# Keeping the four matmuls of a modulation product together in TensorE's order

## The chip, the core and the metric

The kernel runs on one core of a Trainium2 chip. The metric is the device time of one execution in microseconds. Three runs of the kernel before took 3296.96, 3298.60 and 3299.93 us, a median of 3298.6 us. A further execution was taken with the hardware profiler; all rows below are of that one.

## What is computed

The reference runs two blocks of two layers each on 256 latent and 256 context tokens of width 2048: sliding-window attention and latent attention (MLA) in the first block, a mixer of pooling and an RWKV recurrence and then full attention in the second. Each of the four layers is modulated by a condition vector. For the latent tokens it is `c`, for the context tokens `c_ctx`:

```python
shift, scale, gate = jnp.split(cond @ ada_w[i] + ada_b[i], 3, axis=-1)      # cond = silu(c), width 2048
h = rmsnorm(x, norm_g[i]) * (1.0 + scale) + shift
x = x + gate * o                                                            # o: the layer's mixer
```

(In the second block the weights are `mod_w`, and the norm stands elsewhere.) The change concerns only the product `cond @ ada_w[i]`: two condition vectors of 2048 by a 2048 x 6144 matrix, four times, in fp32.

## The kernel before, in words

**The modulation.** The 6144 columns of a layer are cut into 12 groups of 512, and the 2048 rows into four parts `q` of 512 rows. One part of one group is a tile `mraw` of 128 partitions x 4 x 512 numbers (1 MB), so there are 4 x 12 x 4 = 192 tiles, loaded by 192 DMAs on SP's queue (L240) into three buffers. For each tile TensorE does four matmuls (L260), one for each `j` in 0 to 3. Their stationary operand `cs` has just 32 columns, of which two hold the two conditions, and each writes its own band of 32 partitions of one PSUM bank `mv`; `tile_position=(0, 32 * j)` gives each its own quarter of the columns of TensorE's array. I call the four matmuls of one tile a quad. The trace shows two records for each fp32 matmul: 768 matmuls, 1536 records, eight for a quad. After the last quad of a batch ScalarE copies the bank (`ev`, L267), four small matmuls (L273) sum the bands and turn them, and VectorE adds the bias (`mod`, L279).

**When it runs.** `mod_steps` is a generator; each `next` does one quad. `fill`, called after every weight tile of the big products, takes as many steps as a rate (`PACE`) says, and `need` takes the missing ones before a layer uses its modulation. So quads are strewn over the program, between the matmuls of the layers.

**The big products.** `mm3` multiplies in three parts (L352, L353, L354) of 128 x 512, with weights that ScalarE and VectorE split into a rounded part `whi` (L323) and a rest `wlo` (L324). Their raw tiles are loaded on SP's queue too (L338), in the order of that queue. A recurrence in the RWKV mixer (`chain`, L1418 to L1444) alternates between TensorE and ScalarE or VectorE: each step of it needs what they made of the step before.

**What sets the order.** The program is written once in Python, and a scheduler then orders the instructions of each engine by a simulated run: of those that it holds ready, the one that was written earliest goes first. Engines work through their order strictly, and waits are semaphores. So the four matmuls of a quad stand together in TensorE's order only where nothing that was written earlier became ready, in the simulated run, while they were being placed. In the order before, 151 of the 192 quads stand together and 41 are broken: 40 into two pieces (mostly the first matmul alone and then the three others), one into three. So TensorE comes back for the rest of a quad 42 times.

Of the kernel before, what the change touches and what calls it, by code (L numbers as in the profile page):

```python
# [116 lines left out]
class Net:  # L117
# [125 lines left out]
    def mod_steps(self):  # L243
        nc = self.nc
        for i in range(4):
            if i % 2 == 0:
                self.conditions(i // 2)
            mod, cs = self.mod[i], self.cs
            for gs in MOD_BATCHES[min(i, 1)]:
                pb = self.bank("mv")  # L250
                for n, g in enumerate(gs):
                    for q in range(4):
                        while len(self.mod_ahead) < (self.mod_pool[1] - 1 if self.mod_pool and self.mod_loads else 0):
                            self.mod_load()
                        if not self.mod_ahead:
                            self.mod_load()
                        raw = self.mod_ahead.pop(0)
                        for j in range(4):
                            k = 4 * q + j
                            nc.tensor.matmul(  # L260
                                pb[32 * j : 32 * j + 32, :], cs[:, 32 * k + 30 - 2 * n : 32 * k + 62 - 2 * n], raw[:, j, :],
                                start=(n == 0 and q == 0), stop=(n == len(gs) - 1 and q == 3), tile_position=(0, 32 * j),
                            )
                        self.mod_wait = MOD_LAG
                        yield
                ev = self.t512("ev")
                nc.scalar.copy(ev, pb)  # L267
                for _ in range(MV_LAG):
                    yield
                p2 = self.bank("mv2")  # L270
                c = 2 * len(gs)
                for j in range(4):
                    nc.tensor.matmul(  # L273
                        p2[:, c * j : c * j + c], ev[:, j * P : (j + 1) * P], self.sel[:, :c], start=True, stop=True
                    )
                for n, g in enumerate(gs):
                    bias = self.v("mod_b", i * 48 + g * 4, 4).unsqueeze(2).broadcast_to([P, 4, 2])
                    pv = p2[:, : 4 * c].rearrange("p (j n c) -> p j n c", j=4, c=2)[:, :, n, :]
                    nc.vector.tensor_tensor(mod[:, g * 4 : (g + 1) * 4, :], pv, bias, op=ALU.add)  # L279
                    self.mod_done.add((i, g))  # L280
                yield
# [1759 lines left out]
```

## Time and profile before

| | |
|---|---|
| median of three runs | 3298.6 us |
| profiled execution | 3288.34 us, its span 3286.3 us |
| TensorE matmul busy | 3117.3 us, 95% of the span |
| VectorE, ScalarE, GpSimd busy | 2101.0, 1481.1, 351.2 us |
| L260 matmul records | 1536 |
| TensorE's granted clock, mean | 0.983 of full |

"Busy" is the time in which at least one instruction of the engine is at work. Matmuls are pipelined, so a record's own duration is longer than the time after which the next one starts; where a cost is wanted, the start of one row is to be compared with the start of the next. "PEld" is the loading of the stationary operand, "SPq" is SP's queue of DMAs, "idle before" is time in which an engine waited, and behind the arrow stands what ended it.

### The profile page before, as it was taken

To read this page: it belongs to the slowest core of one execution; us is meant where nothing else is said; L and a number is where in the kernel's file an instruction comes from. 1 tells how busy PE (TensorE), PEld (TensorE's weight loads), DVE (VectorE), ACT (ScalarE), POOL (GpSimd) and SP (SyncE) were. 2 spreads that over 40 slices of the span, in tenths; PEclk is the share of its full clock that TensorE was granted. 3 is DMA by queue.
4 is the path that set the end of the run, shared out by engine and by line. 5 is a ranking of instruction groups with operands and counts; after the bars stand their busy time and mean duration, and the time that the engine had idled before them with its cause. 6 is when DMAs were issued, how large, how long until landed. Compare 5 with 4: busy or idle time off the path is not lost. (4 is left out here: it accounts for less than half of the span.)

```text
span 3286.3 us, 53227 instructions
## 1 busy us (share of the span) xinstructions
PE 3117.3 (95%) x19762; PEld 2397.2 (73%) x19762; DVE 2101.0 (64%) x4647; ACT 1481.1 (45%) x3233; POOL 351.2 (11%) x536
## 2 busy tenths in 40 slices
PE   5999999999988999999999999999999999899997
PEld 2567777767777788897776676666677768678897
DVE  2446454553376666666777788777787546857766
ACT  2424444442276666653334334333343323646664
POOL 0000000000001111000122222221121101200000
PEclk8999999999999999999999999999999999999999
DMA  8843444348654666766434433334434474543454
GB/s 303 309 165 135 139 137 157 125 174 290 234 165 142 226 208 226 253 228 211 126 98 133 124 125 116 111 103 149 126 109 154 168 253 130 172 140 129 143 180 153
DMA packets 270771, 556.07 MB, mean 169 GB/s; under 512 B 122928, under 2 KB 150704, under 8 KB 244912
## 3 DMA queue, kind: packets, MB, share of 16 engines
q1 hardware_dynamic: 270512, 552.68, 50.8%
q8 instruction: 155, 2.54, 0.3%
q14 instruction: 104, 0.85, 0.1%
HBM read 517.46 MB, written 35.13 MB: 168 GB/s over the span
## 5 line engine op out<-in xcount | busy, mean ns | idle before, releaser
L324 DVE TENSOR_TENSOR wlo<-raw,whi 128x512 fp32r<-128x512 f32 (+2 forms) x1000 | 660.3, 668 | 572.7 <-ACT whi L323 538.3
L352 PE MATMUL a<-hhi,whi 128*128 128x512 f32 (+1 forms) x2752 | 972.8, 355 | 16.6 <-ACT whi L323 11.9
L323 ACT CAST whi<-raw 128x512 fp32r<-128x512 f32 (+2 forms) x1000 | 593.0, 599 | 815.4 <-PE a L353 470.8
L353 PE MATMUL a<-hlo,whi 128*128 128x512 f32 (+1 forms) x2752 | 947.3, 345 | 0.0
L354 PE MATMUL a<-hhi,wlo 128*128 128x512 f32 (+1 forms) x2752 | 940.0, 347 | 4.5 <-DVE wlo L324 4.3
L352 PEld LDWEIGHTS a<-hhi,whi 128*128 128x128 f32 x2752 | 525.6, 191 | 145.2 <-issue 45.0
L354 PEld LDWEIGHTS a<-hhi,wlo 128*128 128x128 f32 x2752 | 522.6, 191 | 63.5 <-DVE wlo L324 10.2
L353 PEld LDWEIGHTS a<-hlo,whi 128*128 128x128 f32 x2752 | 526.3, 191 | 46.0 <-issue 2.2
L456 POOL TENSOR_TENSOR rs<-st,mhalf 128x4 f32<-128x4 f32 (+3 forms) x109 | 145.7, 1337 | 1683.3 <-DVE st L453 1666.3
L260 PE MATMUL mv<-mraw,cs 128*32 128x512 f32 x1536 | 258.3, 629 | 16.5 <-DMA mraw<-mod_w 16.2
L352 PE MATMUL a<-whi,hhi 128*128 128x512 f32 (+1 forms) x672 | 260.6, 398 | 13.4 <-ACT sq L613 5.9
L353 PE MATMUL a<-wlo,hhi 128*128 128x512 f32 (+1 forms) x672 | 262.7, 391 | 1.4 <-DVE wlo L324 1.1
L354 PE MATMUL a<-whi,hlo 128*128 128x512 f32 (+1 forms) x672 | 258.8, 388 | 0.0
L1427 POOL TENSOR_SCALAR SD<-SV,DL 64x64 f32<-64x64 f32 x224 | 130.0, 580 | 468.7 <-DVE SV L1438 452.4
L352 PEld LDWEIGHTS a<-whi,hhi 128*128 128x128 f32 x672 | 126.1, 190 | 71.2 <-issue 18.6
L353 PEld LDWEIGHTS a<-wlo,hhi 128*128 128x128 f32 x672 | 127.9, 190 | 31.5 <-DVE wlo L324 7.3
L354 PEld LDWEIGHTS a<-whi,hlo 128*128 128x128 f32 x672 | 127.6, 190 | 25.4 <-issue 0.8
L565 ACT ACTIVATE pr<-sc,nm 128x512 f32<-128x512 f32 (+1 forms) x128 | 81.1, 633 | 90.2 <-DVE nm L562 66.7
L1430 ACT COPY SV<-chain 64x64 f32<-64x64 f32 x128 | 26.6, 208 | 184.5 <-DVE SV L1429 178.8
L556 DVE TENSOR_REDUCE mx<-sc 128x1 f32<-128x512 f32 (+1 forms) x128 | 78.9, 617 | 37.8 <-PE sc L766 15.9
L260 PEld LDWEIGHTS mv<-mraw,cs 128*32 128x32 f32 x1536 | 37.0, 110 | 87.8 <-issue 50.3
L1444 ACT COPY y<-chain 64x64 f32<-64x64 f32 x256 | 52.9, 207 | 98.2 <-PE chain L1441 87.8
(379 smaller groups left out, 4690.6 us busy)
## 6 DMA issues: line engine op xcount, KB each, us to landing
mraw<-mod_w SPq DMA_DIRECT2D x192, 1024.0 KB, 4.9
raw<-od_in SPq DMA_DIRECT2D x88, 512.0 KB, 3.6
raw<-swa_in SPq DMA_DIRECT2D x72, 512.0 KB, 3.6
raw<-ev_rkv SPq DMA_DIRECT2D x64, 384.0 KB, 3.4
raw<-ev_in SPq DMA_DIRECT2D x48, 512.0 KB, 3.9
raw<-swa_out SPq DMA_DIRECT2D x40, 512.0 KB, 5.6
raw<-ev_out SPq DMA_DIRECT2D x40, 512.0 KB, 3.6
raw<-mla_g SPq DMA_DIRECT2D x64, 256.0 KB, 3.3
```

The costliest lines, as they stand in the source:

```text
L260: nc.tensor.matmul(pb[32 * j : 32 * j + 32, :], cs[:, 32 * k + 30 - 2 * n : 32 * k + 62 - 2 * n], raw[:, j, :], start=(n == 0 and q == 0), ...
L323: nc.scalar.copy(whi, raw)
L324: nc.vector.tensor_tensor(wlo, raw, whi.bitcast(F32), op=ALU.subtract)
L352: mm(out, ah, bh, start=first, stop=False, skip_group_check=shared)
L353: mm(out, ah, bl, start=False, stop=False, skip_group_check=shared)
L354: mm(out, al, bh, start=False, stop=last, skip_group_check=shared)
L456: self.nc.gpsimd.tensor_tensor(dst, stv, mv, op=ALU.pow)
L556: nc.vector.reduce_max(mx, sc, axis=AX.X)
L565: nc.scalar.activation(pr[:, :n], sc, AF.Exp, scale=scale, bias=nm, accum_out=sm)
L1427: nc.gpsimd.tensor_scalar(SD[r_], SV[r_, hh, c, :], DL[r_, c : c + 1], None, ALU.mult)
L1430: nc.scalar.copy(SV[half[1], 1, c, :], ps[half[1], P : P + L])
L1444: nc.scalar.copy(y[r_, c, :], blk(3 * P, hh))
```

## The change

```diff
                         for j in range(4):
                             k = 4 * q + j
-                            nc.tensor.matmul(
-                                pb[32 * j : 32 * j + 32, :], cs[:, 32 * k + 30 - 2 * n : 32 * k + 62 - 2 * n], raw[:, j, :],
-                                start=(n == 0 and q == 0), stop=(n == len(gs) - 1 and q == 3), tile_position=(0, 32 * j),
-                            )
+                            with self.tc.high_priority(0 if j == 0 else None):
+                                mm = nc.tensor.matmul(
+                                    pb[32 * j : 32 * j + 32, :], cs[:, 32 * k + 30 - 2 * n : 32 * k + 62 - 2 * n], raw[:, j, :],
+                                    start=(n == 0 and q == 0), stop=(n == len(gs) - 1 and q == 3), tile_position=(0, 32 * j),
+                                )
+                                if j:
+                                    self.tc.keep_in_program_order(mm)
```

No instruction is added or taken away. `high_priority(0)` leaves the first matmul of a quad where it was; `high_priority(None)` gives the three others the priority of the program's very start, so that nothing else goes ahead of them once they may go; `keep_in_program_order` puts each behind the matmul that was written just ahead of it, an order alone, without a wait. In the order after, all 192 quads stand together. Lines below the change have numbers higher by four (L352 is L356 there), and the matmul of the modulation is L262.

The first place is on TensorE, in the first attention layer, where a quad (`mv<-mraw`) stood on both sides of a triple of a big product (`a<-whi`). Before:

```order
L354 MATMUL a_303_1677<-whi_308_1683,hlo_79 128x512
L260 MATMUL mv_161_967<-mraw_258_1549,cs_28_185 32x512
L352 MATMUL a_304_1678<-whi_308_1683,hhi_78 128x512
L353 MATMUL a_304_1678<-wlo_309_1684,hhi_78 128x512
L354 MATMUL a_304_1678<-whi_308_1683,hlo_79 128x512
L260 MATMUL mv_161_967<-mraw_258_1549,cs_28_185 32x512 x3
L352 MATMUL a_303_1677<-whi_310_1703,hhi_78 128x512
```

After:

```order
L358 MATMUL a_303_1677<-whi_308_1683,hlo_79 128x512
L262 MATMUL mv_161_967<-mraw_258_1549,cs_28_185 32x512 x4
L356 MATMUL a_304_1678<-whi_308_1683,hhi_78 128x512
L357 MATMUL a_304_1678<-wlo_309_1684,hhi_78 128x512
L358 MATMUL a_304_1678<-whi_308_1683,hlo_79 128x512
L356 MATMUL a_303_1677<-whi_310_1703,hhi_78 128x512
```

The three have moved ahead of the triple, to the first; all else stands as it did.

The second place is on TensorE in the RWKV layer, among the steps of the recurrence (`chain`). Before:

```order
L1432 MATMUL chain_5356_25845<-SV_5296_25434,BKs_5276_25358 128x128
L260 MATMUL mv_5246_25167<-mraw_5362_25881,cs_2058_9283 32x512
L1441 MATMUL chain_5356_25845<-SV_5296_25434,qb1_14957 128x128
L260 MATMUL mv_5246_25167<-mraw_5362_25881,cs_2058_9283 32x512 x3
L352 MATMUL a_5287_25391<-hhi_78,whi_5374_25972 128x512
L353 MATMUL a_5287_25391<-hlo_79,whi_5374_25972 128x512
L1418 MATMUL chain_5356_25845<-SV_5296_25434,AQ_5216_24983 128x128
```

After:

```order
L1436 MATMUL chain_5356_25845<-SV_5296_25434,BKs_5276_25358 128x128
L262 MATMUL mv_5246_25167<-mraw_5362_25881,cs_2058_9283 32x512 x4
L1445 MATMUL chain_5356_25845<-SV_5296_25434,qb1_14957 128x128
L356 MATMUL a_5287_25391<-hhi_78,whi_5374_25972 128x512
L357 MATMUL a_5287_25391<-hlo_79,whi_5374_25972 128x512
L1422 MATMUL chain_5356_25845<-SV_5296_25434,AQ_5216_24983 128x128
```

Between the chain's step L1441 and its next, L1418, there are now two matmuls instead of five.

The scheduler's simulated run comes out a little differently, and so other rows move too. The third place is on SP's queue in the RWKV layer: loads of the modulation (`mraw`) and of the layer's weights (`raw`). Before:

```order
L338 DMA raw_4008_18626<-ev_rkv 128x768
L240 DMA mraw_3994_18553<-mod_w 128x2048
L240 DMA mraw_4039_18777<-mod_w 128x2048
L1188 DMA tl_4018_18685<-lora_14738 128x512
L1188 DMA tl_4019_18686<-lora_14738 128x512
L1488 DMA oscr_80<-yo_3606_16536 128x512
L240 DMA mraw_4077_18964<-mod_w 128x2048
```

After:

```order
L240 DMA mraw_3994_18553<-mod_w 128x2048
L240 DMA mraw_4039_18777<-mod_w 128x2048
L240 DMA mraw_4077_18964<-mod_w 128x2048
L1192 DMA tl_4018_18685<-lora_14738 128x512
L1492 DMA oscr_80<-yo_3606_16536 128x512
L1192 DMA tl_4019_18686<-lora_14738 128x512
L240 DMA mraw_4119_19211<-mod_w 128x2048
L1297 DMA nscr_3999_18577<-NT_3981_18474 64x8x64
L342 DMA raw_4008_18626<-ev_rkv 128x768
```

Four loads of the modulation now stand ahead of the weights `raw_4008`; `mraw_4119` stood 21 instructions further back before. This is the largest such move on SP; over the whole program 13 of the 192 loads move by more than two places, 7 by more than five.

## Rows read from the trace of the kernel before

**Rows 1.** The core's row: span and mean granted clock

```profile
core 0: 3286.3 us, clock 0.983
```

**Rows 2.** The page: TensorE's busy time, share of the span, records

```profile
PE 3117.3 (95%) x19762; PEld 2397.2 (73%) x19762; DVE 2101.0 (64%) x4647; ACT 1481.1 (45%) x3233; POOL 351.2 (11%) x536
```

**Rows 3.** The page: the chain that ended last, shares by engine

```profile
PE 27%; DVE 5%; ACT 2%; DMA 1%; issue 1%; POOL 1%; SPq 0%; POOLq 0%; DVEq 0%; ACTq 0%
```

**Rows 4.** Two stretches: length, busy time by engine (records), clock, DMA share, GB/s

```profile
230.00:720.00 490.00, 482.36 (x2429) 357.97 (x2428) 260.49 (x652) 220.72 (x486) 17.05 (x16) 1.00 0.41 139
...
1500.00:2400.00 900.00, 869.54 (x6200) 614.62 (x6199) 697.27 (x1619) 340.86 (x860) 193.24 (x334) 0.98 0.41 125
```

**Rows 5.** Costliest groups, matmuls and weight loads: busy, mean ns | idle before, releaser

```profile
L260 PE MATMUL mv<-mraw,cs 128*32 128x512 f32 x1536 | 258.3, 629 | 16.5 <-DMA mraw<-mod_w 16.2
...
L260 PEld LDWEIGHTS mv<-mraw,cs 128*32 128x32 f32 x1536 | 37.0, 110 | 87.8 <-issue 50.3
```

**Rows 6.** Timeline, a quad that stands together: start us, own duration, records

```profile
226.99 1.06 PE L260 MATMUL mv<-mraw,cs 128*32 128x512 f32 x8
227.98 0.50 PE L352 MATMUL a<-whi,hhi 128*128 128x512 f32 x1
```

**Rows 7.** Timeline, the first broken quad, in the first attention layer

```profile
243.68 0.40 PE L354 MATMUL a<-whi,hlo 128*128 128x512 f32 x1
244.00 1.04 PE L260 MATMUL mv<-mraw,cs 128*32 128x512 f32 x2
244.98 0.50 PE L352 MATMUL a<-whi,hhi 128*128 128x512 f32 x1
245.31 0.39 PE L353 MATMUL a<-wlo,hhi 128*128 128x512 f32 x1
245.54 0.40 PE L354 MATMUL a<-whi,hlo 128*128 128x512 f32 x1
245.87 1.06 PE L260 MATMUL mv<-mraw,cs 128*32 128x512 f32 x6
246.86 0.50 PE L352 MATMUL a<-whi,hhi 128*128 128x512 f32 x1
```

**Rows 8.** Timeline, a broken quad among the steps of the recurrence

```profile
2580.23 1.04 PE L260 MATMUL mv<-mraw,cs 128*32 128x512 f32 x2
2581.21 0.49 PE L1441 MATMUL chain<-SV,qb 128*128 128x128 f32 x2
2581.63 1.06 PE L260 MATMUL mv<-mraw,cs 128*32 128x512 f32 x6
2582.61 0.50 PE L352 MATMUL a<-hhi,whi 128*128 128x512 f32 x1
2582.96 0.40 PE L353 MATMUL a<-hlo,whi 128*128 128x512 f32 x1
2583.19 0.38 PE L1418 MATMUL chain<-SV,AQ 128*128 128x128 f32 x2
2583.33 0.48 PE L354 MATMUL a<-hhi,wlo 128*128 128x512 f32 x1
```

**Rows 9.** Timeline, a broken quad while the clock was at half

```profile
2366.59 1.91 PE L260 MATMUL mv<-mraw,cs 128*32 128x512 f32 x2 [1.03 <-DMA mraw<-mod_w]
2368.43 0.79 PE L1270 MATMUL gram<-AQ,BK 64*128 64x128 f32 x2
```

**Rows 10.** Timeline, TensorE and ScalarE: a chain step and the copies of its result

```profile
1807.16 0.49 PE L1441 MATMUL chain<-SV,qb 128*128 128x128 f32 x2
...
1807.68 0.42 ACT L1444 COPY y<-chain 64x64 f32<-64x64 f32 x2 [1.67 <-PE chain L1441]
```

**Rows 11.** TensorE's waits: us in total, times, longest

```profile
PE a L352 <- ACT whi L323: 13.9, 12, 3.4
...
PE chain L1418 <- ACT y L1444: 4.2, 13, 0.6
```

**Rows 12.** Waits of SP's queue: us in total, times, longest

```profile
SPq L240 <- PE mv L260: 680.5, 163, 16.4
```

## The prediction

> **What bounds the kernel now.** I read the core's row first: one core, a span of 3286.3 us, the clock at 0.983 of full on the mean [rows 1]. The page's busy times then show TensorE at work for 3117.3 us, 95% of the span; the next, VectorE, has 64% [rows 2]. The chain that ended last agrees: of the shares that it puts to an engine, TensorE has 27 points and the next one 5 [rows 3]. A share of a whole program hides stages, so I cut it: in the first attention layer, 230 to 720 us, TensorE is busy for 482.4 of 490 us; in most of the RWKV layer, 1500 to 2400, for 869.5 of 900, with VectorE at 697.3 [rows 4]. So in the first of them nearly nothing but TensorE's own work sets the time, and in the second it does so too, but with 30.5 us of waits and with a VectorE that is not far behind. What TensorE is spared is worth its time unless it turns into a wait.
>
> **What a piece of a quad costs.** The modulation's matmuls are busy for 258.3 us; a record's mean of 629 ns times 1536 would be 966 us, so they overlap nearly four deep [rows 5]. How, the timeline shows. In a quad that stands together the eight records are done within 1.06 us, and the next matmul starts 227.98 - 226.99 = 0.99 us after the first [rows 6]. In the first broken quad the lone matmul holds TensorE for 244.98 - 244.00 = 0.98 us, and the three others for 246.86 - 245.87 = 0.99 us [rows 7]. One quarter of the array costs as much as four. Joining the two pieces saves one of them.
>
> It saves the way there and back as well. Between matmuls of the big product starts are 245.54 - 245.31 = 0.23 us apart; into the lone matmul it takes 244.00 - 243.68 = 0.32, and from the matmul behind it to the next 245.31 - 244.98 = 0.33 [rows 7]. So a visit costs 0.32 + 0.98 + 0.33 - 2 x 0.23 = 1.17 us.
>
> The page's row gives 258.3 us of busy time for these matmuls, and the rows of the timeline give the start of whatever comes next. The Trainium skill (Trainium Kernel Development and Optimization, Performance Expectations) calls matmul busy time a bad metric, because matmuls are pipelined. By busy time a visit would be worth the lone record's 1.04 us, and 42 of them 43.7 us; from start to start they are 49.1. The trace agrees with the rule here, and I use starts.
>
> Against the whole idea stands another rule. The rows show one quarter at 0.98 us and four at 0.99. The Trainium skill (TensorE: Matmul & The Clock Gate, The mechanism) says that a weight load overlaps with running matmuls only if its group of rows differs, and the four matmuls of a quad use the same rows. By that rule the loads of the three that join, six records of 110 ns [rows 5], would stand in the open, 0.66 us for each rest, and 49.1 us would shrink by 42 x 0.66 to 21.4. The trace disagrees, since 0.99 us leaves no room for them; 49.1 stays.
>
> **The sum.** No instruction comes or goes; 41 broken quads with 42 rests become 41 whole ones. The rests, counted in the order and found again in the timeline, are 11 in the first attention layer (the first of them in [rows 7]), 3 in the MLA layer, and 28 from 1526 us on, in the RWKV layer and its end.
>
> *The 14 in the first two layers.* Big matmuls stand on both sides, and waits are rare: 14 x 1.17 = 16.4 us.
>
> *The 28 in the RWKV layer.* Nineteen of the rests stand next to a step of the recurrence. There a visit costs more. In [rows 8], from the chain's L1441 to the big matmul behind the rest it takes 2582.61 - 2581.21 = 1.40 us, and from that to the next 0.35. Without the rest the first would be as from a chain step to a big matmul, 2583.33 - 2583.19 = 0.14, and the second 0.23: a saving of 1.38, less 0.01 for the larger quad ahead, 1.37 us. 19 x 1.37 = 26.0, and the nine others 9 x 1.17 = 10.5. One rest ran at half clock, behind the lone matmul of [rows 9], which took 1.84 us instead of 0.98: another 0.9. Sum 37.4 us.
>
> *What comes late next.* Of these 37.4 us a part turns into waits, since the rest was the cover for a copy. After L1441, ScalarE copies its result in two pieces that end 1807.68 + 0.42 - 1807.16 = 0.94 us after its start [rows 10], and the chain's next step L1418 needs them. In the order after, two big matmuls stand between: 0.14 + 0.23 + 0.23 = 0.60 us. So L1418 waits for 0.34 us or a little more, say 0.4, where before it seldom waited: 13 times, 4.2 us in all [rows 11]. While it waits, everything behind it on TensorE waits, since the engine goes strictly by its order. I take 0.4 for each of the 28, since the nine others stand in a layer with waits of the same kind: 11.2 us. This term is the least known. Its bounds are 0 (the scheduler has put other work into the gap) and all 37.4 (every rest was a cover for something that is due no sooner); 0.4 is what the nearest row gives.
>
> *What moves besides.* SP's queue has waited for these very matmuls for 680.5 us in 163 waits, since a load must wait for the last matmul on its buffer [rows 12]; the last one now comes sooner, so this wait shrinks. Behind it stand the weights. TensorE waits for split weights for 13.9 us in all [rows 11], so a little may be gained there; I put it at nothing, as its cover, a TensorE with other work to do, stays. The first matmul of a quad waits for the same load as before, and the three tied to it need nothing that the first did not; the ties add no wait. The other moves in the order, some hundreds of places by a few rows, I put at nothing, with either sign.
>
> Total: 16.4 + 37.4 - 11.2 = 42.6 us, so 3288.3 us of the profiled execution becomes 3245.7. The median of the runs lies 10.3 us above the profiled execution, and I carry this over: 3298.6 - 42.6 = 3256.0 us. The likeliest case has its own range of some 10 us to either side, for the size of the waits and the moved rows: 3246 to 3266.
>
> **The rivals.**
>
> *All of it is kept* (0.14). The scheduler filled each gap that it made, and nothing waits: 16.4 + 37.4 = 53.8 us, 3245 us. For it: TensorE has big matmuls in store in nearly every stretch. Against it: the second place shown of the order has nothing new between L1441 and L1418.
>
> *The RWKV layer gives nothing back* (0.16). The recurrence, not TensorE's sum of work, paces that layer, and each rest taken out becomes a wait of its size. Then only the 14 count: 3298.6 - 16.4 = 3282 us. For it: VectorE at 697 of 900 us and 30.5 us of waits [rows 4]. Against it: those waits are 3.4% of the layer; a layer paced by the recurrence would show more.
>
> *The clock* (0.03). The quads' records fill TensorE's time, and with fewer of them the gaps before chain steps widen. The clock fell to half behind a 1.03 us wait in [rows 9]; on the mean 0.983 [rows 1] is 3286.3 x 0.017 x 2 = 112 us at half, which cost 56. To eat 43 us, time at half would have to grow by three quarters: no change, 3298. Against it: a 1 us wait is not rare, and most of them left the clock alone.
>
> *The three are joined and it does not count* (0.02): the order is as wanted but the chip does not run them beside each other: 3298. The 151 quads that already stand together speak against it.
>
> *Weights held up on SP* (0.05), the slower one. Its place is the third one shown of the order: four loads of the modulation ahead of `raw_4008`, and a few like it in the same layer. If `mraw_4119` waits on its buffer, until the quad of `mraw_3994` is done, all weights behind it wait as long; the longest such wait was 16.4 us [rows 12]. TensorE then runs out of split weights. Three of these in the open cost 49.2 us: 3256.0 + 49.2 = 3305 us. It decides from the third on, since 2 x 16.4 is less than 42.6. Against it: 680.5 us of such waits stood beside just 13.9 us of TensorE's waits for weights [rows 11], so nearly none was in the open.
>
> **How the numbers follow.** The likeliest case has 0.60. Its time is the forecast: 3256 us. The range runs from 3244, just under the case where all is kept, to 3282, where the RWKV layer gives nothing; outside lie the clock, the unjoined quads and SP's queue (0.10 together) and the third of the two edge cases that overshoots (0.10). A measurement of this kernel can tell about 0.2%, 6.6 us, from no change. Faster by more: the first three cases, 0.90. Within it: 0.05, from the clock and the quads that do not overlap. Slower: 0.05, from SP's queue.
>
> **What would show it.** The modulation's matmul row must fall from 258.3 us busy by some 42 us with the same 1536 records, and the timeline must show them by eights, 0.99 us to the next start, in the RWKV layer too. In the first attention layer the work from 230 to 720 us must end some 12 us sooner, 11 x 1.17. TensorE's waits for `y` (L1444) and the other copies of the recurrence must grow, by about 11 us. I am wrong if the modulation's busy time falls and the span does not, with the waits grown by as much (the second rival), if waits for `whi` grow by tens of microseconds (SP), or if the mean clock falls to about 0.97.

## The result, and the profile after

| | before | after |
|---|---|---|
| median of the runs | 3298.2 us (4) | 3262.0 us (4) |
| lowest to highest | 3297.0 to 3299.9 | 3257.4 to 3263.0 |
| profiled execution, its span | 3288.34, 3286.3 us | 3257.43, 3255.6 us |
| records of the modulation's matmuls | 1536 | 1536 |

The kernel became 36.2 us faster, a ratio of 0.9887 [0.987, 0.9904]. Run once more at the end, beside other kernels, it took 3266.0 us against 3296.2, a ratio of 0.99 [0.9887, 0.9914]. The forecast was 3256 us, with 3244 to 3282 as its range. Gains below are worked out from the ratios, times the runs of before, and brackets hold 95% intervals.

The first lines of the page after, which answer to [rows 1 to 3], and the modulation's row, which answers to [rows 5]:

```profile
core 0: 3255.6 us, clock 0.982
...
PE 3080.4 (95%) x19762; PEld 2391.1 (73%) x19762; DVE 2102.0 (65%) x4647; ACT 1479.0 (45%) x3233; POOL 346.8 (11%) x536
...
PE 20%; DVE 3%; DMA 1%; ACT 1%; issue 1%; POOL 0%; SPq 0%; POOLq 0%; ACTq 0%; DVEq 0%
...
L262 PE MATMUL mv<-mraw,cs 128*32 128x512 f32 x1536 | 214.4, 634 | 18.9 <-DMA mraw<-mod_w 18.8
```

The reader is to see four things. The number of records is the same. The modulation's busy time fell by 258.3 - 214.4 = 43.9 us. TensorE's as a whole fell by 3117.3 - 3080.4 = 36.9. And what TensorE doesn't work, span less busy, rose from 169.0 to 175.2 us. The clock stayed, at 0.982 against 0.983.

The first attention layer, from the same matmul to the same matmul, first in the trace before and then in that after (columns as in [rows 4]):

```profile
228.00:728.07 500.07, 489.39 (x2459) 363.38 (x2456) 266.11 (x661) 226.09 (x495) 17.05 (x16) 1.00 0.42 140
```

```profile
228.26:718.37 490.11, 479.58 (x2460) 362.40 (x2457) 265.73 (x660) 225.30 (x494) 17.03 (x16) 0.99 0.42 143
```

The same work takes 490.11 us instead of 500.07, so 10.0 us less, where 12 were forecast. Why not more, the place of [rows 7] shows. TensorE's timeline after:

```profile
243.95 0.40 PE L358 MATMUL a<-whi,hlo 128*128 128x512 f32 x1
244.27 1.06 PE L262 MATMUL mv<-mraw,cs 128*32 128x512 f32 x8
245.27 0.50 PE L356 MATMUL a<-whi,hhi 128*128 128x512 f32 x1
245.61 0.39 PE L357 MATMUL a<-wlo,hhi 128*128 128x512 f32 x1
...
246.07 0.40 PE L356 MATMUL a<-whi,hhi 128*128 128x512 f32 x1
246.61 0.30 PE L648 MATMUL tr<-ident,hr 128*128 128x128 f32 x1
...
249.74 0.50 PE L648 MATMUL tr<-ident,hr 128*128 128x128 f32 x2 [0.83 <-DVE hr L637]
```

And before, the last two of these:

```profile
247.20 0.27 PE L644 MATMUL tr<-ident,hr 128*128 128x128 f32 x1
...
249.47 0.50 PE L644 MATMUL tr<-ident,hr 128*128 128x128 f32 x2
```

The quad stands together, and the next matmul starts 1.00 us after it. Count from the matmul ahead of the quad. The one of the next triple, ahead of the first transpose `tr`, came 246.86 - 243.68 = 3.18 us later before [rows 7] and comes 246.07 - 243.95 = 2.12 us later now: 1.06 saved. The transpose then starts 0.54 us after it instead of 0.34, and the second transpose shown waits 0.83 us for VectorE's `hr`: it came 249.47 - 243.68 = 5.79 us later before, and comes 249.74 - 243.95 = 5.79 later now. At this one place all was given back.

In the recurrence it is kept. TensorE's timeline after, at the place of [rows 8]:

```profile
2549.87 1.06 PE L262 MATMUL mv<-mraw,cs 128*32 128x512 f32 x8
2550.87 0.49 PE L1445 MATMUL chain<-SV,qb 128*128 128x128 f32 x2
2551.11 0.49 PE L356 MATMUL a<-hhi,whi 128*128 128x512 f32 x1
2551.43 0.39 PE L357 MATMUL a<-hlo,whi 128*128 128x512 f32 x1
2551.87 0.49 PE L1422 MATMUL chain<-SV,AQ 128*128 128x128 f32 x2
```

From the chain's step L1445 to its next, L1422, it takes 2551.87 - 2550.87 = 1.00 us; before it took 2583.19 - 2581.21 = 1.98. L1422 starts 0.44 us after the big matmul ahead of it, where the next big one would have come after 0.23. So it waits for some 0.2 us, but nearly all of that lies under that matmul's record, which is 0.39 us long: 0.05 us are left between the two, and only these count as waiting. TensorE's waits after, which answer to [rows 11], and SP's, to [rows 12]:

```profile
PE a L356 <- ACT whi L327: 16.5, 16, 3.2
...
PE chain L1426 <- DVE Rp L1425: 6.8, 14, 0.9
...
PE yt L1475 <- ACT Z L1399: 5.8, 4, 1.5
...
PE yt L1475 <- DVE y L1464: 5.4, 5, 2.4
...
PE chain L1422 <- ACT y L1448: 1.7, 6, 0.6
```

```profile
SPq L240 <- PE mv L262: 612.4, 153, 16.8
```

The wait for `y` in the chain did not grow; it fell from 4.2 to 1.7 us.

### The profile page after: what moved, and what is told of

Read it like the earlier page. It is cut to its first block, busy times and chain, and to the rows that moved or that the text cites. A ratio compares the mean times of both kernels' runs of the same rounds, so it can differ in the third digit from the quotient of the medians.

```text
span 3255.6 us, 53230 instructions
## 1 busy us (share of the span) xinstructions
PE 3080.4 (95%) x19762; PEld 2391.1 (73%) x19762; DVE 2102.0 (65%) x4647; ACT 1479.0 (45%) x3233; POOL 346.8 (11%) x536
## 5 line engine op out<-in xcount | busy, mean ns | idle before, releaser
L356 PE MATMUL a<-hhi,whi 128*128 128x512 f32 (+1 forms) x2752 | 975.2, 355 | 18.9 <-ACT whi L327 12.4
L356 PEld LDWEIGHTS a<-hhi,whi 128*128 128x128 f32 x2752 | 527.1, 192 | 122.6 <-ACT whi L327 44.1
L356 PE MATMUL a<-whi,hhi 128*128 128x512 f32 (+1 forms) x672 | 260.6, 397 | 14.6 <-ACT sq L617 5.9
L262 PE MATMUL mv<-mraw,cs 128*32 128x512 f32 x1536 | 214.4, 634 | 18.9 <-DMA mraw<-mod_w 18.8
L356 PEld LDWEIGHTS a<-whi,hhi 128*128 128x128 f32 x672 | 126.4, 190 | 64.1 <-ACT whi L327 12.4
L576 ACT ACTIVATE pr<-pr,rc 128x512 f32<-128x512 f32 (+1 forms) x128 | 85.7, 669 | 19.6 <-DVE rc L575 19.3
```

Of the source, the lines that this page charges most:

```text
L262: mm = nc.tensor.matmul(pb[32 * j : 32 * j + 32, :], cs[:, 32 * k + 30 - 2 * n : 32 * k + 62 - 2 * n], raw[:, j, :], start=(n == 0 and q = ...
L356: mm(out, ah, bh, start=first, stop=False, skip_group_check=shared)
L576: nc.scalar.activation(pr[:, :n], pr[:, :n], AF.Copy, scale=rc)
```

## The experiments

**What tells joining from moving.** The change does two things: it joins 41 broken quads, and it lets the scheduler move other rows. To part them I wrote the order of a kernel, engine by engine, into the program as a list, and tied each instruction behind the one before in it, an order without a wait. In that list single quads can be joined or broken and nothing else moves. The edit is the same for all of these kernels, only the list differs:

```diff
         st.finish(LAT, (1, 1, 2, 2, 2, 2, 2, 2, 1, 1))
+    hold(tc)
...
```

(`hold`, added further down, goes through one list for each engine and ties every instruction to the one listed ahead of it.)

**Joined, nothing else moved.** The list is the order of before, with the rests of the 41 quads put behind their first piece.

> Every engine's order is held to that of the kernel before, instruction by instruction; only the three others of each of the 41 broken quads stand behind the first. Theory A (joining is worth what the sum said, 42.6 us, and the rows that the scheduler moved besides cost the 6 to 7 us that are missing): about 3255 us, 43 us under the kernel before and some 7 us under the changed kernel's 3262. Rival B (the moved rows cost nothing, waits behind the joined quads are larger than the 11.2 us that I took): as the changed kernel, 3262 us within 3. Rival C (the scheduler's new order helps, since it fits the joined quads): slower than the changed kernel, 3267 us or more.

Measured: 3255.8 us, 0.9867 [0.9841, 0.9894]. It ran a second time beside the kernels of the second group below:

> The kernel with all else held to the order of before and the quads joined, once more, beside the kernel with 14 quads moved and on the same chip: 3256 us. Its distance to the kernel before should again be 43 us within 8.

Measured: 3258.8 us, 0.988 [0.9864, 0.9895]. So joining alone is worth 43.9 and 39.6 us, where the sum of the prediction says 42.6. In the profile of the first, TensorE's busy time is 3074.7 of 3254.8 us, 42.6 less than before; span less busy is 180.1 us, 11.1 more than before:

```profile
PE 3074.7 (94%) x19762; PEld 2391.0 (73%) x19762; DVE 2101.6 (65%) x4647; ACT 1479.8 (45%) x3233; POOL 352.2 (11%) x536
```

**Moved, not joined.** The list is the order of after, with the 41 quads broken again.

> Every engine's order is held to that of the changed kernel; only the 41 quads that were broken before are broken again, the first matmul, then the three instructions that followed the quad, then the three others. So it has the moved rows without the joining. Theory A (moved rows cost 6 to 7 us): 3305 us, that much above the kernel before. Rival B (they cost nothing): 3298 us within 3. Rival C (they help): 3293 us or less.

Measured: 3306.5 us, 1.0016 [1.0001, 1.0031], so 5.3 us over before. Joining within the order of after is thus worth the difference of the ratios, 1.0016 - 0.9887, or some 42.5 us, and 38 with the second measurement of after, 0.99. The moved rows by themselves cost 5.3 us, with an interval, 0.3 to 10.2, that nearly reaches zero.

**A part of the quads.** Only the first 14 joined, in the first two layers, and only the 27 behind them.

> Order held to that of the kernel before; only the first 14 broken quads, those of the two attention layers, are joined. The sum said 14 x 1.17 = 16.4 us with no wait: 3282 us. The changed kernel's trace shows about 12 us gone at the end of these layers, with waits for copies of VectorE behind two of the quads and a longer stretch at half clock: by that 3286 us.

> Order held to that of the kernel before; only the last 27 broken quads with 28 rests, those from the RWKV layer on, are joined. The sum said 37.4 - 11.2 = 26.2 us: 3272 us. If the recurrence paces that layer (the second rival of the prediction), 3298 us. If the waits behind the joined quads are what is missing in the changed kernel, about 3278 us. With the joined quads of the first layers this should add up to the kernel in which all are joined.

Measured: 3285.5 us for the first, 0.996 [0.9945, 0.9974], 13.2 us gained; 3273.8 for the others, 0.9921 [0.9897, 0.9946], 26.1 us gained. The intervals are 8.6 to 18.1 and 17.8 to 34.0 us. Together 39.3, against 43.9 and 39.6 for both at once: the parts add up, as far as these intervals tell.

**More quads broken.** In the order of before, 97 of its whole quads are broken as well.

> The other way round: order held to that of the kernel before, and 97 quads that stood together there are broken too, the first matmul, the two instructions that followed the quad, then the three others: 138 broken quads, 139 rests instead of 42. If a rest costs TensorE 1.17 us and the way there and back is part of it, the 97 cost 97 x 1.17 = 113 us: 3412 us. If only the matmul's own 0.98 us counts: 3394 us. If a good part of such visits lies beside waits (the second rival), 3355 us or less. If the four do not gain from standing together, 3298 us.

Measured: 3394.1 us, 1.0287 [1.0268, 1.0305], 94.7 us lost, or 0.98 us for each, 0.91 to 1.04 by the interval. The two profiles differ by 3394.4 - 3286.3 = 108.1 us, 1.11 for each: TensorE's busy time grew by 114.6 us and span less busy fell by 6.5, at a clock of 0.981 against 0.983. So the price of a rest holds far outside of the change in the main, a little under 1.17 us. That the way there and back is what is missing from it is not shown.

**The tie alone.** All four matmuls keep the priority of their place in the order of writing; each is only tied behind the one before. Against after:

```diff
-                            with self.tc.high_priority(0 if j == 0 else None):
+                            with self.tc.high_priority(0):
```

> One part of the change alone: the three others are tied behind the first in the scheduler's order, but keep their own priority instead of that of the program's start. In the order this breaks 63 quads into 130 pieces, 67 rests instead of 42. By the price of a rest, 25 more cost 25 x 1.17 = 29 us less some waits: about 3322 us, plus or minus 8 for the moved rows. If the tie were what helps: 3262 us as in the changed kernel.

Measured: 3321.2 us, 1.0069 [1.0055, 1.0083], so 22.8 us slower than before. Tied like this, the quads are broken more often: the order has 129 whole ones and 67 rests instead of 42. The two pages, of this kernel and of the one with 97 more broken, show it as more busy time with the same number of records:

```profile
L262 PE MATMUL mv<-mraw,cs 128*32 128x512 f32 x1536 | 286.9, 638 | 20.6 <-DMA mraw<-mod_w 20.3
```

```profile
L260 PE MATMUL mv<-mraw,cs 128*32 128x512 f32 x1536 | 364.5, 636 | 25.4 <-DMA mraw<-mod_w 25.0
```

25 more rests cost 28.6 us of busy time in the one, 97 cost 106.2 in the other: 1.1 us each. What joins the quads in the change is the priority, not the tie: with the priority and without the tie the program comes out instruction for instruction as in after.

**All four in one quarter.** Is it the quarters, side by side, that make four as cheap as one, or only that the four stand together? All four write the same band, from the same quarter of the array. Against after:

```diff
-                                    pb[32 * j : 32 * j + 32, :], cs[:, 32 * k + 30 - 2 * n : 32 * k + 62 - 2 * n], raw[:, j, :],
-                                    start=(n == 0 and q == 0), stop=(n == len(gs) - 1 and q == 3), tile_position=(0, 32 * j),
+                                    pb[0:32, :], cs[:, 32 * k + 30 - 2 * n : 32 * k + 62 - 2 * n], raw[:, j, :],
+                                    start=(n == q == j == 0), stop=(n == len(gs) - 1 and q == j == 3), tile_position=(0, 0),
```

(The copy `ev` and the sum behind it then take 32 rows. The expectation says that nothing else is changed; but the scheduler moves other rows here too, so the price is better read from a quad than from the total.)

> The kernel after, with all four matmuls of a quad in the first quarter of the array and the first band of the bank, summed there by the accumulation flags; the four still stand together, nothing else is changed in the program. Theory A (what a joined quad saves is that its four quarters run beside each other): the four now stand one after the other, a quad takes some 4 x 0.98 = 3.9 us instead of 0.99, and 192 x 2.93 = 563 us come on top, less what hides under the loads at the start of the program (the first 32 quads or so wait for their loads): 3700 to 3825 us. Theory B (what it saves is the way to another kind of matmul and back, and the records that stand side by side would overlap anyway): a quad keeps about 1 us, and the time stays at 3262 us.

Measured: 3671.4 us, 1.1151 [1.1108, 1.1194], 409 us over the median of after, and 416 by the ratios. That the four stand together is not enough: they must also lie in different quarters, with their bands of the bank. The run changes quarter and band at once and does not part the two. A quad in its timeline, and the page's row:

```profile
241.68 3.62 PE L262 MATMUL mv<-mraw,cs 128*32 128x512 f32 x8
245.23 0.51 PE L356 MATMUL vp<-vw,hhi 128*128 128x512 f32 x1
```

```profile
L262 PE MATMUL mv<-mraw,cs 128*32 128x512 f32 x1536 | 701.4, 601 | 8.8 <-DMA mraw<-mod_w 8.6
```

A quad takes 3.55 us instead of 1.00, and the busy time grew by 701.4 - 214.4 = 487 us. My 3.9 us for a quad was too much, since a lone matmul's 0.98 holds something that four in a row pay once; so the time came out under the range that I gave. Of the 487 us, 417 reach the end of the profile. Two things make up for the others. TensorE waits less: span less busy is 130.8 us here and 175.2 in after. And the clock's mean is 0.992 here and 0.982 in after, so by an estimate the time lost to it is 3672.5 x 0.008 = 29 us instead of 3255.6 x 0.018 = 59.

**Quads put into gaps.** Could the give-back be avoided by putting quads where TensorE waits? In the joined order, 14 quads are moved later, to stand just ahead of a matmul that waited.

> The held order with all quads joined, and 14 quads moved later, each to just ahead of a matmul that waited 0.57 to 1.99 us in the trace of that kernel. If a quad fills a wait at no cost, 14 x its 1.17 us or the wait if that is shorter, 12 us in all: 3244 us. If the waits are only pushed on (what the matmul waits for starts later by as much, or the later release of the load's buffer holds up SP's queue): 3256 us or more.

Measured: 3282.2 us, 0.9957 [0.9943, 0.9971], 23 us over the median of the joined order beside it, and 25 by the ratios. The timeline of TensorE and of SP's queue shows the largest single loss:

```profile
2234.30 1.06 PE L260 MATMUL mv<-mraw,cs 128*32 128x512 f32 x8
2245.73 3.67 PE L1165 MATMUL pool<-pm,pwt 128*128 128x512 f32 x4 [10.37 <-DMA pwt<-pool_w]
```

```profile
2214.91 0.38 SPq L1161 DMA_DIRECT2D pwt<-pool_w  x1
...
2235.42 0.33 SPq L240 DMA_DIRECT2D mraw<-mod_w  x1
...
2241.96 0.33 SPq L1161 DMA_DIRECT2D pwt<-pool_w  x1
```

And the same three loads in the joined order of the same group:

```profile
2209.20 0.38 SPq L1161 DMA_DIRECT2D pwt<-pool_w  x1
...
2215.45 0.33 SPq L240 DMA_DIRECT2D mraw<-mod_w  x1
...
2224.19 0.33 SPq L1161 DMA_DIRECT2D pwt<-pool_w  x1
```

The load into the buffer of the quad at 2234.30 could go only behind that quad, at 2235.42; from the `pwt` ahead of it that is 20.5 us, in the joined order 6.3. The next load of `pwt` stood behind it on SP's queue, and behind two stores of `oscr`, for whose landing it waited another 3.6 us; and TensorE waited 10.37 us for it. That is the mechanism of the prediction's slower rival. The rest of the loss is not at this place: in the profiles span less busy grew by 13.4 us in all, and TensorE's busy time by 9.3 with the clock at 0.979 instead of 0.982. The change itself did not set it off: in after, TensorE's waits for `whi` are 16.5 us, against 13.9 before.

**Where do the moved rows cost?** From 1785 us on the joined order took 146 us for what took 150 in after, between the same two matmuls. It is the third place shown of the order, so I looked for the 5 us there: the joined order with this stretch alone as in after, the order of after with this stretch alone put back, and after once more, all on one chip.

> The order of before with the 41 broken quads joined (as in the version that was held to it), and only one stretch put in the order of after, on all five engines: from about 1755 to 1930 us, the third place shown of the order, where four loads of the modulation stand ahead of the weights raw_4008. In that version the stretch from 1785 us on took 146 us, in after the same work took 150. Theory A (the moved rows cost some 5 us, and nearly all of it here): the stretch takes 150 us again, and the time is 4 us over the joined version: 3261 us. Theory B (the moved rows cost it in many places by a little, or the 5 us are the spread of the runs): the stretch takes 146 to 147 us and the time stays at 3256 to 3259.

> The other way round: the order of after everywhere, and only that stretch in the order of before, with its quads joined. Theory A: the stretch takes 146 us instead of 150, and 4 us of the 5 that the moved rows cost come back: 3258 us against 3262 of after. Theory B: 3262, as after.

> The kernel after, once more, beside the other two on one chip, so that differences of 4 us can be read. Theory A: 3262 us, 4 over the version with the stretch put back, and as far above before's joined order as the version with the stretch alone. Theory B: the three lie within 2 us of each other.

Measured: 3264.9 us, 0.9901 [0.9887, 0.9916]; 3266.6, 0.9901 [0.9886, 0.9916]; and 3266.0, 0.99 [0.9887, 0.9914]. The first took 6 us and more over the joined order's two medians, as theory A says or worse, and not B's 3256 to 3259; but the joined order itself was measured on other chips. The second gave nothing back, against A. The stretch itself, from the same matmul to the same, in the joined order, again in the joined order, in after, with the stretch as in after, and with the stretch put back:

```profile
1785.00:1931.00 146.00, 141.00 (x1074) 102.55 (x1073) 113.33 (x268) 57.88 (x152) 37.65 (x61) 1.00 0.42 125
```

```profile
1784.07:1933.29 149.22, 144.56 (x1074) 104.44 (x1073) 113.41 (x268) 57.86 (x152) 37.70 (x61) 0.97 0.42 122
```

```profile
1786.43:1936.64 150.21, 141.31 (x1063) 102.09 (x1062) 115.41 (x272) 57.70 (x151) 32.02 (x60) 0.97 0.39 115
```

```profile
1792.36:1942.41 150.05, 140.70 (x1063) 102.02 (x1062) 113.98 (x269) 57.72 (x151) 31.68 (x59) 0.98 0.39 115
```

```profile
1792.76:1939.28 146.52, 141.55 (x1076) 102.95 (x1075) 113.91 (x269) 57.74 (x152) 37.70 (x61) 1.00 0.42 124
```

With the order of after the stretch takes 150 us (three executions of three, the one not shown 149.95) and TensorE's waits, length less busy, are 8.9 to 9.6 us of it. With the order of before they are 4.7 to 5.0. But that order took 149.22 us, too, in one execution, when the clock was at 0.97 and TensorE's busy time 3.6 us longer with it. So the place does cost about 4 us of waits, and the clock can cost as much on top. Nearly all of these waits stand before the matmuls `yt` (L1475, or L1471): they wait for VectorE's `y` and ScalarE's `Z` for 4.2 us of the stretch in after, and for 0.4 in the joined order. The work is not quite the same: in the order of after one quad of the modulation lies outside of the stretch, 48 records instead of 56. What came behind it in the kernel with the stretch put back, and in after once more, again for the same work:

```profile
2034.24:2347.54 313.30, 302.31 (x2186) 217.36 (x2186) 244.14 (x570) 119.59 (x306) 67.22 (x123) 0.96 0.41 120
```

```profile
2036.65:2343.36 306.71, 295.17 (x2186) 212.22 (x2186) 244.09 (x570) 119.72 (x306) 67.86 (x123) 0.99 0.41 123
```

There the one with the stretch put back lost 6.6 us, at a clock of 0.96 against 0.99: what it had gained was gone in a later stretch. So neither theory comes out whole. The stretch is slower in the order of after, as A says, but putting it back doesn't bring the difference of the totals back; the three lie within 2 us of each other, as B says, at a mean clock of 0.980 over the runs of the one put back and of 0.981 for the other two. That moved rows cost some 5 us in all rests on the order of after with broken quads, and on the medians of the joined order and of after; which of the rows do is open.

The clocks of the runs show that these two legs are not one price. The order of after with broken quads had the same mean clock as the runs of before beside it, 0.981; its 5.3 us are not the clock's. But the joined order had 0.983 on the mean of its runs, at both measurements, and after had 0.981, at both. Among the runs of before, a clock lower by 0.001 went with 1.6 to 2.5 us more (a straight line through each group of them). By this estimate, 3 to 4 of the 6.2 us between the joined order and after are time at half clock, and not waits; and of the 43.9 and 39.6 us of the joined order as much is clock that it gained over before. Whether the order sets the clock of the whole, or only of single places, no run shows.

## Why the prediction held, and where it did not

*What bounds the kernel.* It held: what TensorE is spared arrives at the end, 43.9 and 39.6 us for a sum of 42.6, some 3 to 4 us of it by the clock, which the sum did not have.

*The price of a piece.* It held. Four quarters take 1.00 us, one takes 0.98, four in the same quarter 3.55. The Trainium skill (TensorE: Matmul & The Clock Gate, The mechanism) says that weight loads overlap with running matmuls only where the group of rows differs; by that rule the joined quads would have kept 21.4 us. The measured 39.6 and 43.9 speak against it for these quads, as the rows of before had.

*The 14 in the first two layers, 16.4 us.* Perhaps a little too much: 13.2 us by the kernel with only these joined, with an interval of 8.6 to 18.1, which holds 16.4 too. In the trace the first layer gained 10.0 of 11 x 1.17 = 12.9 us (the prediction says some 12). "Waits are rare" was the weak word: at the first broken quad of all, the transpose behind it was due no sooner, and took everything back.

*The 28 in the RWKV layer, 37.4 less 11.2 us.* The net held: 26.2 forecast, 26.1 measured for these alone, with an interval of 17.8 to 34.0, so that it agrees to a tenth is luck. The place of [rows 8] shows 0.98 us net where 1.37 - 0.4 = 0.97 was forecast, and there two errors cancel. Behind the chain's step the two big matmuls take 0.24 and 0.32 us from start to next start in after, not 0.14 and 0.23; so without a wait the stretch would be some 0.79 us, the saving 1.98 - 0.79 = 1.19 and not 1.37, and the wait 0.2 and not 0.4. The sign that I named for the wait failed, too. TensorE's waits for `y` did not grow by 11 us, because a wait of some 0.2 us, as at that place, hides under the end of the record ahead. In the joined order the time without a busy record grew by 11.1 us, as much as the term, yet only 3.0 of it in the chain's waits for `Rp`, `y` and `SV` (14.6 us before, 17.6 there). At the one place worked out here the 0.4 was about twice too large; that the 11.2 is right as a sum is not shown. Only the net of the group is.

*What moves besides, nothing.* This is the step that held worst: "The other moves in the order, some hundreds of places by a few rows, I put at nothing, with either sign." Alone they cost 5.3 us [0.3, 10.2], and after stands 6.2 us over the joined order at the first measurement of each (3262.0 and 3255.8). The forecast missed by 6.0 us, which lies inside the 10 us that it gave itself, and this term has that size. That it is the whole miss is not shown, since 3 to 4 us of the 6.2 went with the clock. Both signs are in it: the stretch from 1785 us on lost 4 us, while from 2335.93 to 2400.64 us the order of after took 64.71 us for what took 70.00 in the joined one. The two rows, joined and after:

```profile
2330.00:2400.00 70.00, 64.94 (x474) 48.04 (x475) 53.11 (x121) 23.82 (x61) 14.83 (x23) 0.87 0.38 114
```

```profile
2335.93:2400.64 64.71, 59.73 (x477) 42.92 (x477) 51.75 (x121) 23.93 (x62) 13.08 (x23) 0.96 0.38 121
```

Here it is the clock, 0.87 of full against 0.96, near the place of [rows 9] (1.00 would be a clock of 2.4 GHz throughout, and its other level is 1.2). It goes with the order: from the first `x` (L1404, or L1408) to the big matmul that waits for VectorE's `g`, the two executions of the joined order took 69.06 and 69.12 us at 0.87, and the two of after 63.64 and 63.59 at 0.97.

*The carrying over to the median.* The profiled execution after lies 4.6 us under its median, that of before 10.3 under the one it was held against. So the two profiles differ by 30.9 us and the medians by 36.2. Two executions of after itself, profiled in two groups of runs, had spans of 3255.6 and 3263.8 us at the same mean clock, 0.982. So a single execution of this kernel tells nothing below 8 us on the total; places in it are more exact.

*The rivals.* "All of it is kept" would have shown 53.8 us for the joined order, which its intervals (35.0 to 52.4, and 34.6 to 44.9) leave out, the first by little. "The RWKV layer gives nothing back", where each rest taken out becomes a wait, would have shown no gain for the 28; they gained 26.1. The clock stayed at 0.982. SP's queue did not hold up weights in after, but the quads put into gaps set this off, at 10.4 us for a single load.

## What to carry to other kernels

Small matmuls that run side by side in quarters of the array are worth that only where they stand together in the engine's order: look there, not in the source, and price each piece from start to start of the rows beside it. When a scheduler makes the order, part the wanted change from what else it moves by holding the order and changing one thing; here the rest ate about a seventh of what was wanted, in part by way of the clock. The version that does only the wanted thing, the order of before held and its quads joined, is the fastest that ran (3255.8 and 3258.8 us; after 3262.0 and 3266.0), by about as little as can be told here.

## What the runs showed of the hardware

- Four fp32 matmuls of 128 x 512 with 32 columns each took 1.00 us from start to next start in four quarters and 3.55 us in one quarter and one band, a ratio of 3.55. The Trainium skill (TensorE: Matmul & The Clock Gate, Measured speedup vs the span model) has 2.38 for three columns; no run here has three.
- A lone one took 0.98 us between other matmuls, but 3.55 / 4 = 0.89 in a row of its kind. Going into a quarter and out again cost 0.1 us each way: starts 0.32 and 0.33 us apart, instead of 0.23 [rows 7].
- The clock falls to half in short spells (a lone matmul took 1.84 us there [rows 9] instead of 0.98), at places that differ with the order and from one execution to the next. The same stretch in the same order had 1.00 and 0.97, and took 146.0 and 149.2 us; another had 0.87 in both executions of one order and 0.97 in both of the other. The slower kernel with all four matmuls in one quarter, with TensorE busy for 3541.7 of 3672.5 us, had 0.992.
